# A fixed order for the first projection, the first FFN pair and the step into the down-projection, decays and residual tiles loaded earlier, and longer gaps in the weave of a one-core encoder layer

## Chip, core and metric

The kernel runs on one core of a Trainium2 chip. The metric is the device time of one execution in microseconds (us). The core has TensorE (PE, matmuls; its weight loads are listed as PEld), VectorE (DVE), ScalarE (ACT), GpSimd (POOL) and SyncE (SP). Each runs its own instructions in the order in which they were written into its list; semaphores hold an instruction until what it needs is there. SP, ACT and POOL also issue DMA transfers, and an issue stands in the engine's line like any other instruction.

## What is computed

One layer on 512 tokens of width 2048, in float32: a token mixer with eight gated-delta heads beside a gated short convolution, cross-attention to 256 memory tokens with four heads, and a SwiGLU FFN whose up-projection is followed by a causal convolution of width 3. Cut to what matters here:

```python
def gdn_group(proj, conv_w, a_log, dt_bias, out_gain):
    qkv = silu(causal_dwconv(proj[..., :3 * W], conv_w))
    q, k = l2norm(...), l2norm(...)
    beta = sigmoid(b_raw)
    g = -exp(a_log) * softplus(a_raw + dt_bias)
    o = gated_delta_rule(q, k, v, g, beta)      # decays exp(g_i - g_j), triangular solve, state over 4 chunks
    return rmsnorm(o, out_gain) * silu(z)

def memory_xattn(h, mem_n, w_q, w_k, w_v, w_o):
    q, k, v = h @ w_q, mem_n @ w_k, mem_n @ w_v
    return softmax(q @ k.T * scale) @ v @ w_o

def conv_ffn(h, w_up, conv_w, w_down):
    u = causal_dwconv(h @ w_up, conv_w)
    gate, up = u[..., :D_FF], u[..., D_FF:]
    return (silu(gate) * up) @ w_down
```

Each of the three parts has an RMSNorm ahead of it and a residual add behind it.

## The kernel before

Activations lie transposed, features on the 128 partitions and tokens along the row. A float32 product is made of three reduced ones: every operand is a rounded part (hi, made by an ACT cast) and a rest (lo, a DVE subtraction), and PE runs hi x hi, hi x lo and lo x hi into one bank of PSUM (`mm3`, L152 to L155). Weights come in pieces of 128 x 1024: SP loads a piece into one of five buffers (wst), ACT casts it to whi, DVE makes wlo (three buffers each); `wpiece` (L132) does this. So behind every matmul stands a chain of load, cast and subtraction, and an engine that stands in its line holds back the weights of everything behind it. The activations share one pool of 64 tiles (`T`). PSUM has eight banks, three in pool `PM` and five in `PG`.

The order on each engine is made by a scheduler from the program, except inside `manual_schedule`, where the named engines follow the order of the code.

The stages in order, with the times at which PE works on them:

- 0 to 74 us, keys of the memory (`mem_proj(w_xk)`, L340): 16 columns of 16 blocks, two to a tile (psk). The first tile alternates between two banks. The sum of squares of the memory tokens is built by ACT (squares) and POOL (macc, L240), and turned around by two matmuls on it (psn, L231), called from `mem_norm` behind the third tile (L326). ACT, DVE and SP follow the code for the first weight pieces (L273); PE does not. To about 400 us follow the folded query weights, the memory's values and the folded output weights.
- 400 to 1120 us, the mixer's input projection, three kinds of 16 blocks of 24 matmuls. For each head h, `qkvz` (L463) projects q, k, v and z, and behind v opens a chain (`delta`, L485) of small transposes, matmuls and vector work. `weave` and `tick` (L171 to L183) scatter the chain between the projection's matmuls: each `yield cost, gap` tells how much clock the step took and how long the next one waits, in units of about one microsecond (a block of three matmuls counts 0.65). A chain loads its row of decays (gb, L489, a DMA on POOL), forms the decay tile dt (L492), inverts a triangular matrix in steps of 16, 32 and 64 (tiles psa, bt, ps1, ps2, L566 to L593), runs over four chunks with a state (L595 to L621) and norms its output (psn, L629). The small tiles bk, nk, ss, vn come from pool `sp` with two buffers each.
- 1120 to 1395 us, the mixer's output projection and the attention scores; 1395 to 1486 us, the attention's output (`out_proj`, L748), whose 16 tiles are prepared for the FFN by `up_prepare` (L766).
- 1486 to 2382 us, the up-projection. Each of 44 pairs (a gate tile and an up tile of 128 features) is made with seven products instead of eight (a Strassen-like scheme, L836 to L884): 24 matmuls of 256 columns each, in the order r = 1, 2, 6, 5, 7, 3, 4. The weights of products 5, 6, 7 and 3 are sums of weight blocks: s1 = w21 + w22 (a second, adding DMA on POOL, L840), s3 = w21 - w11, s2 = s1 - w11 and w12 - s2 (DVE, L857 and L865). Behind the products come norm, convolution, gate, and a DMA of the hidden tile to memory (L884).
- 2390 to 2900 us, the down-projection, four groups of four output tiles (`GN`), each over 11 steps of four hidden tiles: 48 matmuls of 512 columns a step. ACT, DVE and POOL follow the code (L914). Hidden tiles (L903) and weights are split two steps or two pieces ahead. At a group's end the residual is loaded (L943, POOL), added to the bank (L944, DVE), squared (ACT) and accumulated (L240, POOL). Then the last norm and the output, to 2925 us.

Of the kernel before, what the change touches and what calls it, by code (L numbers as in the profile page):

```python
# [15 lines left out]
P = 128  # L16
S = 512
# [51 lines left out]
def trunk(ctx: ExitStack, tc: tile.TileContext, g):  # L69
# [269 lines left out]

    kts = mem_proj(g["w_xk"], True)  # L340

# [67 lines left out]
    def gates(ps):  # L409
# [17 lines left out]
        nc.vector.scalar_tensor_tensor(gr, gr, 0.0, tmp1, op0=ALU.max, op1=ALU.add)  # L427
        na = cpool.tile([P, H], F32, tag="na", name="na")
        nc.scalar.activation(na, col(C_ALOG, 8), AF.Exp)
        nc.vector.scalar_tensor_tensor(gr, gr, -1.0, rep4(na), op0=ALU.mult, op1=ALU.mult)  # L430
# [53 lines left out]

    def delta(h, q, k, v, z):  # L485
        q4, k4, v4_ = v4(q), v4(k), v4(v)

        gb = T("gb")
        nc.gpsimd.dma_start(v4(gb), gc_d[:, h, :].unsqueeze(0).broadcast_to([P, 4, P]))  # L489
        dt = T("dt")  # L490
# [79 lines left out]
        nc.scalar.copy(bt, psa)  # L570
        yield 0.5, 4.5

        for s in (32, 64):
# [3 lines left out]
            for ev, od in pairs:  # L577
                for j in range(4):
                    nc.tensor.matmul(v4(ps1)[od, j, ev], v4(nt)[ev, j, od], v4(bt)[ev, j, ev], start=True, stop=True)
# [11 lines left out]
            for ev, od in pairs:  # L591
                nc.vector.tensor_tensor(v4(pt)[ev, :, od], v4(pt)[ev, :, od], v4(ps2)[ev, :, od], op=ALU.subtract)
            yield 0.7, 2.8  # L593

        pso = PG("pso")  # L595
        st = None
        for j in range(4):
            r = v4(v)[:, j]
            if j:
                pr = PG("pr")  # L600
                nc.tensor.matmul(pr[:, :P], v4(ke)[:, j], st, start=True, stop=True)
                nc.vector.tensor_tensor(r, r, pr[:, :P], op=ALU.subtract)
                yield 0.3, 1.0
            pv = PG("pv")
            nc.tensor.matmul(pv[:, :P], v4(pt)[:, j], r, start=True, stop=True)
            vn = sp.tile([P, P], F32, tag="vn", name=nm("vn"))
            nc.scalar.activation(vn, pv[:, :P], AF.Identity, scale=bk[:, j : j + 1])
# [176 lines left out]

    turn()
    xs1 = None
    for idx in range(KT):
        n = (idx % 2) * HK + idx // 2
        out_proj(n, 0)
        out_proj(n, 1)  # L790
        ps = x2s[-1][0]
# [26 lines left out]

    def sums(s, i):

        if i == 0:
            return wp.tile([P, 1024], F32, tag="wst", name=nm(s), bufs=WST)
        return us.tile([P, 1024], F32, tag="us", name=nm(s))

    def product(ps, w, r, first):

        hi, lo = w
        for k in range(HK):
# [4 lines left out]
            nc.tensor.matmul(ps, lo[:, c], xh, start=False, stop=k == HK - 1, skip_group_check=True)  # L833

    r2 = []
    for i in range(NF):  # L836
        w11, w12, w21, w22 = (g["w_up"][q] for q in ((i, 0), (i, 1), (NF + i, 0), (NF + i, 1)))
        s1 = sums("s1", i)
        nc.sync.dma_start(s1, w21)
        nc.gpsimd.dma_start(s1, w22, accum_op=ALU.add)  # L840
        a11, a22, a12 = raw(w11), raw(w22), raw(w12)
        s3 = sums("s3", i)
        nc.scalar.activation(s3, a11, AF.Identity, scale=-1.0)
        nc.gpsimd.dma_start(s3, w21, accum_op=ALU.add)
        tt = nc.vector.tensor_tensor
        w1 = wsplit(a11)
        px = PG("px")[:, :S2]
        product(px, w1, 1, True)
        tq, tz = T("tq"), T("tz")
        nc.scalar.copy(tq[:, LO], px)  # L850
        w2 = wsplit(a12)
        py = PM("py")[:, :S2]
        product(py, w2, 2, True)
        ug, uu = T("ug"), T("uu")
        tt(ug[:, LO], py, tq[:, LO], op=ALU.add)
        s2 = sums("s2", 1)
        tt(s2, s1, a11, op=ALU.subtract)  # L857
        product(px, wsplit(s2), 6, False)
        nc.scalar.copy(tq[:, HI], px)
        pz = PG("pz")[:, :S2]  # L860
        product(pz, wsplit(s1), 5, True)
        nc.scalar.copy(tz[:, LO], pz)
        product(px, wsplit(s3), 7, False)
        tt(uu[:, HI], px, tz[:, LO], op=ALU.add)
        tt(a12, a12, s2, op=ALU.subtract)  # L865
        product(pz, wsplit(a12), 3, False)
        tt(ug[:, HI], pz, tq[:, HI], op=ALU.add)
        product(px, wsplit(a22), 4, False)
        if not r2:
            r2.append(rstd_rows([acc2]))  # L870
        tt(ug, ug, r2[0], op=ALU.mult)
        tt(uu[:, LO], px, r2[0][:, LO], op=ALU.mult)
        tt(uu[:, HI], uu[:, HI], r2[0][:, HI], op=ALU.mult)
        cvs = []
        for u, t in ((ug, i), (uu, NF + i)):
            cv = T("ucv")
            cc = C_FCONV + 3 * t
            nc.scalar.activation(cv, u, AF.Identity, scale=col(cc + 2))
            for a in (1, 2):
                nc.vector.scalar_tensor_tensor(cv[:, a:], u[:, : S - a], col(cc + 2 - a), cv[:, a:], op0=ALU.mult, op1=ALU.add)  # L880
            cvs.append(cv)
        nc.scalar.activation(cvs[0], cvs[0], AF.Silu)
        tt(cvs[0], cvs[0], cvs[1], op=ALU.mult)
        nc.scalar.dma_start(hid_d[i], cvs[0])  # L884

# [23 lines left out]
    def w_split(p):  # L909
        if p < 2 * len(steps):  # L910
            gq, c = steps[p // 2]
            ws[p] = wpiece(g["w_dn"][c, gq * GN // 2 + p % 2])

    with tc.manual_schedule(engines={mybir.EngineType.Activation, mybir.EngineType.DVE, mybir.EngineType.Pool}):  # L914
        for i in range(2):
            hid_load(i)
        for i in range(2):
            for k in range(FC):
                hid_split(i, k)
            w_split(i)  # L920
        for i, (gq, c) in enumerate(steps):
# [17 lines left out]
            if c == nc_ - 1:  # L939
                for q in range(GN):  # L940
                    n = gq * GN + q
                    x2 = T("x3")
                    nc.gpsimd.dma_start(x2, x2_d[n])  # L943
                    nc.vector.tensor_tensor(x2, pss[q], x2, op=ALU.add)  # L944
# [95 lines left out]
```

## Time and profile before

| | |
|---|---|
| time, median of three runs | 2926.73 us (2925.67 to 2928.3) |
| the profiled execution: time, span | 2926.86 us, 2925.0 us |
| PE busy, share of the span | 2832.6 us, 97% |
| mean granted clock of TensorE | 0.985 |
| DVE, ACT, POOL busy | 62%, 46%, 12% |
| DMA, mean over the span | 162 GB/s |

The span reaches from the first to the last instruction of the profiled execution. In lists of waits, `PE psd L153 <- ACT whi L142` means that PE's matmul of line 153 into psd waited for ACT's write of whi in line 142. In timelines a row gives start and duration in us, engine, line, operation, result and operands, and in brackets the idle time before it and what ended it. The granted clock is the share of full speed that TensorE was given.

### The profile page before, as it was taken

What the parts mean: (1) busy time and instruction counts of PE and PEld (TensorE: products, weight loads), DVE (VectorE), ACT (ScalarE), POOL (GpSimd) and SP (SyncE); (2) the same over time, 40 slices, a digit from 0 to 9 for tenths busy, and PEclk for the clock granted to TensorE, in tenths of its full rate; (3) what the DMA queues carried; (4) which work ended last, traced back from release to release, by engine and by line L of the source; (5) the groups of instructions that cost most, each with busy time, mean ns of one, the idle gap of its engine ahead of it and who ended that gap; (6) DMA issues with size and microseconds to landing.
All of it is one profiled execution on the core that took longest, in us unless ns stands there. A gap on an engine that the chain in (4) does not pass through costs nothing.

```text
span 2925.0 us, 44163 instructions
## 1 busy us (share of the span) xinstructions
PE 2832.6 (97%) x17521; PEld 2524.7 (86%) x17521; DVE 1820.2 (62%) x2707; ACT 1346.5 (46%) x1887; POOL 354.7 (12%) x438
## 2 busy tenths in 40 slices
PE   7999999999999999999999999999999989999996
PEld 7999888777777888888889999999999988787775
DVE  5435747767764334446678878888788774444344
ACT  5464644434443223235555555555555543433342
POOL 1020001111110000110110000000000021213132
PEclk9999999999999999999999999999999999999998
DMA  6686763323332224446666666666666665546372
GB/s 215 220 283 195 232 203 109 94 85 95 93 105 78 98 95 157 142 149 185 182 179 169 170 174 161 182 167 162 182 166 168 175 212 187 202 154 224 123 243 69
DMA packets 178944, 473.97 MB, mean 162 GB/s; under 512 B 26656, under 2 KB 50608, under 8 KB 178736
## 3 DMA queue, kind: packets, MB, share of 16 engines
q1 hardware_dynamic: 130896, 335.84, 35.1%
q0 software_dynamic: 29984, 102.80, 15.3%
q10 hardware_dynamic: 17856, 32.51, 3.0%
q8 instruction: 137, 2.24, 0.3%
q14 instruction: 71, 0.58, 0.1%
HBM read 427.02 MB, written 44.06 MB: 161 GB/s over the span
## 4 chain that ended last, share of the span: by engine, by line
PE 58%; issue 8%; DVE 3%; DMA 2%; ACT 1%; POOL 1%; ACTq 0%; SPq 0%; DVEq 0%; POOLq 0%
PE px L833 6%; PE px L831 6%; PE px L832 6%; PE psd L155 3%; PE pz L831 3%; PE pz L833 3%; PE pz L832 3%; PE psd L153 3%; PE psd L154 3%; PE pssc L153 3%; PE pssc L155 3%; PE pssc L154 3%; PE psx L154 2%; PE psx L155 2%; PE psx L153 2%
## 5 line engine op out<-in xcount | busy, mean ns | idle before, releaser
L143 DVE TENSOR_TENSOR wlo<-wst,whi 128x1024 fp32r<-128x1024 f32 x404 | 500.8, 1241 | 583.3 <-ACT whi L142 562.4
L142 ACT CAST whi<-wst 128x1024 fp32r<-128x1024 f32 x404 | 423.9, 1050 | 790.5 <-PE psd L154 237.5
L815 ACT CAST whi<-wst 128x1024 fp32r<-128x1024 f32 x176 | 184.4, 1048 | 291.4 <-PE px L832 143.8
L831 PE MATMUL px<-xoh,whi 128*128 128x256 f32 x1056 | 300.0, 284 | 3.9 <-ACT whi L815 3.2
L153 PE MATMUL psd<-hdh,whi 128*128 128x512 f32 (+1 forms) x720 | 280.4, 389 | 21.9 <-ACT whi L142 21.9
L832 PE MATMUL px<-xol,whi 128*128 128x256 f32 x1056 | 299.7, 284 | 0.0
L833 PE MATMUL px<-xoh,wlo 128*128 128x256 f32 x1056 | 299.6, 284 | 0.0
L155 PE MATMUL psd<-hdh,wlo 128*128 128x512 f32 (+1 forms) x720 | 280.2, 389 | 1.3 <-DVE wlo L143 1.2
L154 PE MATMUL psd<-hdl,whi 128*128 128x512 f32 (+1 forms) x720 | 279.6, 388 | 0.0
L816 DVE TENSOR_TENSOR wlo<-wst,whi 128x1024 fp32r<-128x1024 f32 x176 | 215.2, 1223 | 96.9 <-ACT whi L815 55.8
L831 PEld LDWEIGHTS px<-xoh,whi 128*128 128x128 f32 x1056 | 203.7, 193 | 4.3 <-ACT whi L815 3.5
L832 PEld LDWEIGHTS px<-xol,whi 128*128 128x128 f32 x1056 | 203.7, 193 | 0.0
L833 PEld LDWEIGHTS px<-xoh,wlo 128*128 128x128 f32 x1056 | 203.6, 193 | 0.0
L833 PE MATMUL pz<-xoh,wlo 128*128 128x256 f32 x704 | 199.3, 283 | 0.8 <-DVE wlo L816 0.8
L831 PE MATMUL pz<-xoh,whi 128*128 128x256 f32 x704 | 199.5, 283 | 0.2 <-ACT whi L815 0.2
L832 PE MATMUL pz<-xol,whi 128*128 128x256 f32 x704 | 199.4, 283 | 0.0
L153 PEld LDWEIGHTS psd<-hdh,whi 128*128 128x128 f32 x720 | 137.3, 191 | 50.5 <-ACT whi L142 23.3
L815 ACT CAST whi<-s 128x1024 fp32r<-128x1024 f32 x132 | 138.3, 1049 | 86.5 <-PE px L832 62.0
L155 PEld LDWEIGHTS psd<-hdh,wlo 128*128 128x128 f32 x720 | 136.9, 190 | 31.8 <-DVE wlo L143 4.5
L816 DVE TENSOR_TENSOR wlo<-s,whi 128x1024 fp32r<-128x1024 f32 x132 | 161.1, 1222 | 0.4 <-ACT whi L815 0.4
L154 PEld LDWEIGHTS psd<-hdl,whi 128*128 128x128 f32 x720 | 137.0, 190 | 27.3
L153 PE MATMUL psq<-hh,whi 128*128 128x512 f32 x384 | 155.2, 404 | 0.0
(316 smaller groups left out, 7370.2 us busy)
## 6 DMA issues: line engine op xcount, KB each, us to landing
wst<-in_w_up SPq DMA_DIRECT2D x132, 512.0 KB, 4.9
wst<-in_w_mix SPq DMA_DIRECT2D x112, 512.0 KB, 3.5
s<-in_w_up POOLq DMA_DIRECT2D x88, 512.0 KB, 6.4
wst<-in_w_dn SPq DMA_DIRECT2D x88, 512.0 KB, 3.5
hid<-hid_d POOLq DMA_DIRECT2D x176, 256.0 KB, 5.0
s<-in_w_up SPq DMA_DIRECT2D x44, 512.0 KB, 4.9
wst<-in_w_xk SPq DMA_DIRECT2D x32, 512.0 KB, 3.7
wst<-in_w_xq SPq DMA_DIRECT2D x32, 512.0 KB, 4.8
```

The lines of the kernel that those rows point to most:

```text
L142: nc.scalar.copy(hi, st)
L143: nc.vector.tensor_tensor(lo, st, f(hi), op=ALU.subtract)
L153: nc.tensor.matmul(ps, wh, xh, start=first, stop=False)
L154: nc.tensor.matmul(ps, wh, xl, start=False, stop=False)
L155: nc.tensor.matmul(ps, wl, xh, start=False, stop=last)
L815: nc.scalar.copy(hi, t)
L816: nc.vector.tensor_tensor(lo, t, f(hi), op=ALU.subtract)
L831: nc.tensor.matmul(ps, hi[:, c], xh, start=first and k == 0, stop=False, skip_group_check=True)
L832: nc.tensor.matmul(ps, hi[:, c], xl, start=False, stop=False, skip_group_check=True)
L833: nc.tensor.matmul(ps, lo[:, c], xh, start=False, stop=k == HK - 1, skip_group_check=True)
```

## The change

Five places are edited.

1. The first projection is put under `manual_schedule` for PE, and the Exp of the decay coefficients (na) moves from the gates to the start, behind the first square.

```diff
+        na = cpool.tile([P, H], F32, tag="na", name="na")
+        nc.scalar.activation(na, col(C_ALOG, 8), AF.Exp)
...
-    kts = mem_proj(g["w_xk"], True)
+    with tc.manual_schedule(engines={mybir.EngineType.PE}):
+        kts = mem_proj(g["w_xk"], True)
```

What PE's list holds around psn, before (psk is the tiles' bank, mwh and mwl the memory's two parts, macc the squares):

```order
L153 MATMUL psk_313<-mwh_151,whi_316 128x256
L154 MATMUL psk_313<-mwl_152,whi_316 128x256
L155 MATMUL psk_313<-mwh_151,wlo_317 128x256
L231 MATMUL psn_555<-macc,ones 128x256
L153 MATMUL psk_313<-mwh_161,whi_346 128x256
L154 MATMUL psk_313<-mwl_162,whi_346 128x256
L231 MATMUL psn_555<-macc,ones 128x256
L155 MATMUL psk_313<-mwh_161,wlo_347 128x256
L153 MATMUL psk_313<-mwh_161,whi_346 128x256
```

and after, where `x2` stands for two in a row:

```order
L155 MATMUL psk_438<-mwh_183,wlo_532 128x256
L153 MATMUL psk_438<-mwh_183,whi_531 128x256
L154 MATMUL psk_438<-mwl_184,whi_531 128x256
L155 MATMUL psk_438<-mwh_183,wlo_532 128x256
L231 MATMUL psn_559<-macc,ones 128x256 x2
L153 MATMUL psk_594<-mwh_129,whi_597 128x256
L154 MATMUL psk_594<-mwl_130,whi_597 128x256
L155 MATMUL psk_594<-mwh_129,wlo_598 128x256
```

The two matmuls on macc move from behind row 120 of PE's list to behind row 288, and no longer stand between others of the first tile. The first tile's 96 matmuls now alternate between its two banks.

2. A head's decays are loaded by `qkvz` behind the convolution of its first tile (of the third tile for head 0), and nine of the chain's gaps grow, two of them once for each step size and three once for each chunk.

```diff
+            if t == (0 if h else 2):
+                gb = T("gb")
+                nc.gpsimd.dma_start(v4(gb), gc_d[:, h, :].unsqueeze(0).broadcast_to([P, 4, P]))
         z = T("z")
-        weave(delta(h, *out, z), 6.0)
+        weave(delta(h, *out, z, gb), 6.0)
...
-        yield 1.4, 1.0
+        yield 1.4, 2.5
...
-        yield 0, 12.5
+        yield 0, 17.5
...
-        yield 0.5, 4.5
+        yield 0.5, 8.0
...
-            yield 0.5, 2.8
+            yield 0.5, 4.0
...
-            yield 0.7, 2.8
+            yield 0.7, 4.0
...
-                yield 0.3, 1.0
+                yield 0.3, 2.0
...
-            yield 0.3, 1.2
+            yield 0.3, 1.8
...
-            yield 0.6, 1.2
+            yield 0.6, 2.5
...
-        yield 0, 6.0
+        yield 0, 9.0
```

DVE's list where head 2's chain begins (bk_ and nt_ are head 2's, the cv_ that is subtracted from is head 0's, wlo_ are weight pieces, st_ is head 0's state), before, from head 0's last subtraction on:

```order
L602 TENSOR_TENSOR cv_4506<-cv_4506,pr_5442 128x128
L143 TENSOR_TENSOR wlo_5563<-wst_5560,whi_5562 128x1024
L564 TENSOR_TENSOR pt_5422<-xd_5420,mk 128x512
L492 SCALAR_TENSOR_TENSOR dt_5447<-gb_5445,gc,mk 128x128 x4
L530 TENSOR_TENSOR dt_5447<-pskq_5505,dt_5447 128x512
L143 TENSOR_TENSOR wlo_5621<-wst_5618,whi_5620 128x1024
L512 TENSOR_SCALAR ss_5485<-ss_5485 128x4
L520 TENSOR_TENSOR kx_5498<-pskt_5459,kd 128x512
L514 RECIPROCAL bk_5492<-ss_5485 128x4
L515 TENSOR_TENSOR bk_5492<-bk_5492,beta 128x4
L523 SCALAR_TENSOR_TENSOR nt_5500<-pskk_5464,bk_5492,dts_5457 128x128 x4
```

and after:

```order
L604 TENSOR_TENSOR cv_4509<-cv_4509,pr_5575 128x128
L143 TENSOR_TENSOR wlo_5672<-wst_5669,whi_5671 128x1024
L619 SCALAR_TENSOR_TENSOR st_5631<-st_5555,egl,pss_5629 128x128
L604 TENSOR_TENSOR cv_4509<-cv_4509,pr_5651 128x128
L143 TENSOR_TENSOR wlo_5755<-wst_5752,whi_5754 128x1024
L516 RECIPROCAL bk_5471<-ss_5464 128x4
L517 TENSOR_TENSOR bk_5471<-bk_5471,beta 128x4
L525 SCALAR_TENSOR_TENSOR nt_5479<-pskk_5430,bk_5471,dts_5423 128x128 x4
L539 TENSOR_TENSOR nd_5520<-nt_5479,mk 128x512
```

Head 2's reciprocal now follows head 0's last subtraction with one weight piece between them; the same pair of neighbours comes back with the other heads.

3. Around the attention's output the weights are cast one tile ahead (`out_piece`), and the first pair's loads, its first two casts and its two sums of weight blocks are written ahead of the last output tile. The first s2 takes the buffer of w11 in place of one of its own. Later pairs do the same work as before, their loads through `pair_loads`.

```diff
+        if idx == KT - 2:
+
+            a11, a12, a22, s1, s3 = pair_loads(0, lambda t: wp.tile([P, 1024], F32, tag="wst", name=nm(t), bufs=WST))
+            first = [a11, a12, a22, s1, s3]
+        out_proj(0)
+        out_proj(1)
+        if idx == KT - 1:
+            first += [wsplit(a11), wsplit(a12)]
+            tt(a11, s1, a11, op=ALU.subtract)
+            tt(a12, a12, a11, op=ALU.subtract)
```

ACT's list at the last output tile (x_d is the DMA of the residual to memory, xs the scaled tile, xoh its parts for the products, tq a product's copy; the casts from s_ are of sums of weight blocks), before:

```order
L795 DMA x_d<-x_2117_12763 128x512
L239 ACTIVATE sq_12767<-x_2117_12763 128x512
L798 ACTIVATE xs_12770<-x_2117_12763,cols 128x512
L148 CAST xoh_12780<-xs_12770 128x512
L148 CAST xoh_12784<-tc_12772 128x512
L148 CAST xoh_12788<-td_12773 128x512
L850 COPY tq_12837<-px_12812 128x256
L815 CAST whi_12874<-s_2143_12872 128x1024
L815 CAST whi_12904<-s_2128_12796 128x1024
L815 CAST whi_12933<-s_2132_12805 128x1024
```

and after:

```order
L784 CAST b11h_12685<-xs_12751 128x256
L803 CAST whi_12878<-wst_12710 128x1024
L803 CAST whi_12908<-s_2112_12707 128x1024
L840 DMA x_d<-x_2126_12788 128x512
L239 ACTIVATE sq_12792<-x_2126_12788 128x512
L843 ACTIVATE xs_12795<-x_2126_12788,cols 128x512
L148 CAST xoh_12805<-xs_12795 128x512
L148 CAST xoh_12809<-tc_12797 128x512
L148 CAST xoh_12813<-td_12798 128x512
L926 COPY tq_12847<-px_12822 128x256
L803 CAST whi_12937<-s_2116_12716 128x1024
```

Two casts of sums (of s2, which now lies in a wst buffer, and of s1) move ahead of the last tile's square and scaling. In SP's list the load of the second pair's s1 moves from the first place of that pair's loads to the third, behind two weight loads; in DVE's list the second pair's s2 now stands ahead of the sum uu of the first.

4. The last pair and the first steps of the down-projection get one written order on ACT and DVE, and the hidden tiles of the first two steps are loaded behind the last pair's first product.

```diff
+        with tc.manual_schedule(engines={mybir.EngineType.Activation, mybir.EngineType.DVE}):
+            product(px, wsplit(s3), 7, False)
+            tt(a12, a12, s2, op=ALU.subtract)
+            product(pz, wsplit(a12), 3, False)
+            w4 = wsplit(a22)
             for k in range(FC):
...
+                hid_split(0, k)
+            tt(uu[:, HI], px, tz[:, LO], op=ALU.add)
+            product(px, w4, 4, False)
+            w_split(0)
+            tt(ug[:, HI], pz, tq[:, HI], op=ALU.add)
+            w_split(1)
+            gate = gate_half(i, ug)
+            for k in range(FC):
+                hid_split(1, k)
+            up_half(i, px, uu, gate)
```

`gate_half` and `up_half` hold what each pair did before in one piece: norm, convolution (`unit_conv`) and SiLU of the gate, then norm and convolution of the other half, the product and the DMA of the hidden tile.

5. The residual tiles of a group are loaded at its eighth step of eleven, and only added at its end.

```diff
             hid_load(i + 2)
+            if c == NC_ - 4:
+                for q in range(GN):
+                    x3.append(T("x3"))
+                    nc.gpsimd.dma_start(x3[-1], x2_d[gq * GN + q])
...
-                    x2 = T("x3")
-                    nc.gpsimd.dma_start(x2, x2_d[n])
-                    nc.vector.tensor_tensor(x2, pss[q], x2, op=ALU.add)
-                    x3.append(x2)
+                    nc.vector.tensor_tensor(x3[n], pss[q], x3[n], op=ALU.add)
                     if gq < KT // GN - 1:
-                        add_squares(acc3, x2, n == 0)
+                        add_squares(acc3, x3[n], n == 0)
```

On POOL the four loads then stand ahead of the hidden tiles of three further steps, and the group's four accumulations one behind the other.

More of the change, by code (lines that the diff above doesn't have):

```diff
@@ L427, in gates @@
         nc.vector.scalar_tensor_tensor(gr, gr, 0.0, tmp1, op0=ALU.max, op1=ALU.add)
-        na = cpool.tile([P, H], F32, tag="na", name="na")
-        nc.scalar.activation(na, col(C_ALOG, 8), AF.Exp)
         nc.vector.scalar_tensor_tensor(gr, gr, -1.0, rep4(na), op0=ALU.mult, op1=ALU.mult)
@@ L483, in four, with delta @@
             nc.tensor.matmul(v4(ps)[:, j], lhs(j), rhs(j), start=True, stop=True)
-    def delta(h, q, k, v, z):
+    def delta(h, q, k, v, z, gb):
         q4, k4, v4_ = v4(q), v4(k), v4(v)
-        gb = T("gb")
-        nc.gpsimd.dma_start(v4(gb), gc_d[:, h, :].unsqueeze(0).broadcast_to([P, 4, P]))
         dt = T("dt")
@@ L745, in trunk, with out_piece, out_proj @@
     HK = KT // 2
-    x2s = []
-    def out_proj(n, part):
+    x2s, x2w = [], []
+    order2 = [(i % 2) * HK + i // 2 for i in range(KT)]
+    def out_piece():
+        n = order2[len(x2w)]
+        x2w.append(wpiece(mo_d[:, :, n * P : (n + 1) * P].rearrange("k p n -> p k n")))
+    def out_proj(part):
         if part == 0:
-            x2s.append((PM("psx2"), *wpiece(mo_d[:, :, n * P : (n + 1) * P].rearrange("k p n -> p k n"))))
-        ps, hi, lo = x2s[-1]
+            x2s.append(PM("psx2"))
+        ps, (hi, lo) = x2s[-1], x2w[len(x2s) - 1]
         for k in range(4 * part, 4 * part + 4):
@@ L783, in up_prepare, with raw, wsplit, pair_loads @@
             xop[right].append((th[:, HI], tl[:, HI]))
+    tt = nc.vector.tensor_tensor
+    def raw(src):
+        t = wp.tile([P, 1024], F32, tag="wst", name=nm("wst"), bufs=WST)
+        nc.sync.dma_start(t, src)
+        return t
+    def wsplit(t):
+        hi = wp.tile([P, 1024], F32R, tag="whi", name=nm("whi"))
+        lo = wp.tile([P, 1024], F32R, tag="wlo", name=nm("wlo"))
+        nc.scalar.copy(hi, t)
+        nc.vector.tensor_tensor(lo, t, f(hi), op=ALU.subtract)
+        return hi, lo
+    def pair_loads(i, buf):
+        w11, w12, w21, w22 = (g["w_up"][q] for q in ((i, 0), (i, 1), (NF + i, 0), (NF + i, 1)))
+        s1 = buf("s1")
+        nc.sync.dma_start(s1, w21)
+        nc.gpsimd.dma_start(s1, w22, accum_op=ALU.add)
+        a11, a22, a12 = raw(w11), raw(w22), raw(w12)
+        s3 = buf("s3")
+        nc.scalar.activation(s3, a11, AF.Identity, scale=-1.0)
+        nc.gpsimd.dma_start(s3, w21, accum_op=ALU.add)
+        return a11, a12, a22, s1, s3
     turn()
+    out_piece()
     xs1 = None
     for idx in range(KT):
[L788 to L791, printed above, removed]
+        n = order2[idx]
+        if idx + 1 < KT:
+            out_piece()
+        if idx == KT - 2:
[7 more added lines that the diff above has]
+            tt(a12, a12, a11, op=ALU.subtract)
+        ps = x2s[-1]
         x1 = TB("x2")
@@ L805, in trunk, with US @@
     us = ctx.enter_context(tc.tile_pool(name="us", bufs=4, reuse_waits="tile"))
-    def raw(src):
-        t = wp.tile([P, 1024], F32, tag="wst", name=nm("wst"), bufs=WST)
-        nc.sync.dma_start(t, src)
-        return t
-    def wsplit(t):
-        hi = wp.tile([P, 1024], F32R, tag="whi", name=nm("whi"))
-        lo = wp.tile([P, 1024], F32R, tag="wlo", name=nm("wlo"))
-        nc.scalar.copy(hi, t)
-        nc.vector.tensor_tensor(lo, t, f(hi), op=ALU.subtract)
-        return hi, lo
[L819 to L823, printed above, removed]
+    def US(t):
+        return us.tile([P, 1024], F32, tag="us", name=nm(t))
     def product(ps, w, r, first):
@@ L833, in product @@
             nc.tensor.matmul(ps, lo[:, c], xh, start=False, stop=k == HK - 1, skip_group_check=True)
[L835 to L884, printed above, removed]
     NC_ = NF // FC
@@ L912, in w_split, with unit_conv @@
             ws[p] = wpiece(g["w_dn"][c, gq * GN // 2 + p % 2])
-    with tc.manual_schedule(engines={mybir.EngineType.Activation, mybir.EngineType.DVE, mybir.EngineType.Pool}):
[L915 to L920, printed above, removed]
+    r2 = []
+    def unit_conv(u, t):
+        cv = T("ucv")
+        cc = C_FCONV + 3 * t
+        nc.scalar.activation(cv, u, AF.Identity, scale=col(cc + 2))
+        for a in (1, 2):
+            nc.vector.scalar_tensor_tensor(cv[:, a:], u[:, : S - a], col(cc + 2 - a), cv[:, a:], op0=ALU.mult, op1=ALU.add)
+        return cv
@@ new lines, in gate_half, with up_half @@
+    def gate_half(i, ug):
+        tt(ug, ug, r2[0], op=ALU.mult)
+        cv = unit_conv(ug, i)
+        nc.scalar.activation(cv, cv, AF.Silu)
+        return cv
+    def up_half(i, px, uu, gate):
+        tt(uu[:, LO], px, r2[0][:, LO], op=ALU.mult)
+        tt(uu[:, HI], uu[:, HI], r2[0][:, HI], op=ALU.mult)
+        cv = unit_conv(uu, NF + i)
+        tt(gate, gate, cv, op=ALU.mult)
+        nc.scalar.dma_start(hid_d[i], gate)
+    for i in range(NF):
+        if i:
+            a11, a12, a22, s1, s3 = pair_loads(i, US)
+            w1 = wsplit(a11)
+        else:
+            a11, a12, a22, s1, s3, w1, w2 = first
+        px = PG("px")[:, :S2]
+        product(px, w1, 1, True)
+        if i == NF - 1:
+            hid_load(0)
+            hid_load(1)
+        tq, tz = T("tq"), T("tz")
+        nc.scalar.copy(tq[:, LO], px)
+        if i:
+            w2 = wsplit(a12)
+        py = PM("py")[:, :S2]
+        product(py, w2, 2, True)
+        ug, uu = T("ug"), T("uu")
+        tt(ug[:, LO], py, tq[:, LO], op=ALU.add)
+        if i:
+            s2 = US("s2")
+            tt(s2, s1, a11, op=ALU.subtract)
+        else:
+            s2 = a11
+        product(px, wsplit(s2), 6, False)
+        nc.scalar.copy(tq[:, HI], px)
+        pz = PG("pz")[:, :S2]
+        product(pz, wsplit(s1), 5, True)
+        nc.scalar.copy(tz[:, LO], pz)
+        if i < NF - 1:
+            product(px, wsplit(s3), 7, False)
+            tt(uu[:, HI], px, tz[:, LO], op=ALU.add)
+            if i:
+                tt(a12, a12, s2, op=ALU.subtract)
+            product(pz, wsplit(a12), 3, False)
+            tt(ug[:, HI], pz, tq[:, HI], op=ALU.add)
+            product(px, wsplit(a22), 4, False)
+            if not r2:
+                r2.append(rstd_rows([acc2]))
+            up_half(i, px, uu, gate_half(i, ug))
+            continue
+        with tc.manual_schedule(engines={mybir.EngineType.Activation, mybir.EngineType.DVE}):
+            product(px, wsplit(s3), 7, False)
+            tt(a12, a12, s2, op=ALU.subtract)
+            product(pz, wsplit(a12), 3, False)
+            w4 = wsplit(a22)
+            for k in range(FC):
+                hid_split(0, k)
+            tt(uu[:, HI], px, tz[:, LO], op=ALU.add)
+            product(px, w4, 4, False)
+            w_split(0)
+            tt(ug[:, HI], pz, tq[:, HI], op=ALU.add)
+            w_split(1)
+            gate = gate_half(i, ug)
+            for k in range(FC):
+                hid_split(1, k)
+            up_half(i, px, uu, gate)
```

## The prediction

> **What bounds the kernel now.** I start with the page's busy times, because they say how much there is to win at all.
>
> ```profile
> PE 2832.6 (97%) x17521; PEld 2524.7 (86%) x17521; DVE 1820.2 (62%) x2707; ACT 1346.5 (46%) x1887; POOL 354.7 (12%) x438
> ```
>
> TensorE (PE) is busy for 2832.6 of 2925.0 us, so the span is its work plus 92 us of idle time, plus what its throttled clock costs after a pause. No other engine comes near. The change keeps every product, so it can win only in those pauses. The waits of PE name them (total, times, longest).
>
> ```profile
> PE psd L153 <- ACT whi L142: 21.9, 4, 7.8
> PE psn L231 <- POOL macc L240: 7.6, 1, 7.6
> ...
> PE ps L579 <- ACT bt L570: 4.7, 1, 4.7
> PE ps L579 <- DVE bt L590: 3.8, 2, 2.5
> PE px L831 <- ACT whi L815: 3.2, 1, 3.2
> ...
> PE psn L630 <- ACT snh L148: 2.1, 3, 0.8
> ...
> PE psa L568 <- DVE y L635: 1.5, 1, 1.5
> ...
> PE psk L155 <- DVE wlo L143: 0.8, 1, 0.8
> ```
>
> All but the last hold 44.8 us. To see what a pause costs with the slow clock behind it, I count matmuls. In the window view (us; busy time and count of PE, PEld, DVE, ACT, POOL; granted clock; DMA share; GB/s) a stretch without a pause holds 211 matmuls of 256 columns in 25 us (0.119 us each) or 112 of 512 columns (0.223 us each). A stretch that holds fewer has lost the difference times that step.
>
> ```profile
> 25.00:50.00 25.00, 17.43 (x130) 16.87 (x129) 12.92 (x17) 11.04 (x13) 10.12 (x7) 0.86 0.37 121
> 50.00:75.00 25.00, 25.00 (x211) 25.00 (x210) 14.76 (x20) 10.72 (x12) 0.00 (x0) 1.00 0.64 214
> 500.00:600.00 100.00, 99.17 (x561) 80.08 (x561) 74.81 (x210) 40.09 (x67) 7.34 (x7) 1.00 0.32 97
> 600.00:700.00 100.00, 94.31 (x525) 75.32 (x525) 66.32 (x149) 45.78 (x79) 16.92 (x14) 0.97 0.33 95
> 700.00:800.00 100.00, 97.37 (x525) 78.83 (x524) 76.30 (x206) 45.77 (x79) 14.93 (x14) 1.00 0.31 91
> 800.00:925.00 125.00, 120.05 (x671) 94.99 (x669) 81.33 (x215) 48.45 (x79) 10.65 (x10) 0.96 0.30 92
> 1475.00:1500.00 25.00, 21.12 (x110) 17.80 (x109) 19.31 (x28) 15.19 (x23) 6.34 (x6) 0.90 0.52 143
> 1500.00:1525.00 25.00, 23.46 (x187) 23.06 (x186) 17.42 (x24) 15.89 (x21) 2.55 (x3) 0.96 0.70 184
> ...
> 2375.00:2400.00 25.00, 17.11 (x94) 14.66 (x93) 16.82 (x24) 11.59 (x20) 9.08 (x17) 0.80 0.82 279
> 2500.00:2525.00 25.00, 24.23 (x107) 19.71 (x106) 7.79 (x11) 8.07 (x13) 3.90 (x5) 1.00 0.25 84
> 2525.00:2550.00 25.00, 23.96 (x103) 19.20 (x104) 15.44 (x19) 13.44 (x21) 15.31 (x28) 1.00 0.93 353
> 2550.00:2575.00 25.00, 25.00 (x112) 20.71 (x111) 11.73 (x15) 8.96 (x14) 4.79 (x9) 1.00 0.72 251
> 2625.00:2650.00 25.00, 21.61 (x96) 17.57 (x94) 6.84 (x9) 6.65 (x11) 5.33 (x6) 0.97 0.24 72
> 2650.00:2675.00 25.00, 21.51 (x82) 16.98 (x83) 14.25 (x17) 13.77 (x21) 14.10 (x25) 0.82 0.80 300
> 2775.00:2800.00 25.00, 18.43 (x69) 14.19 (x68) 13.23 (x17) 11.69 (x17) 13.64 (x23) 0.80 0.66 244
> ```
>
> **Part A, the first projection in program order.** PE reaches the sum of squares of the memory tokens (psn) after 120 matmuls and stands, since POOL is still adding the squares.
>
> ```profile
> 34.31 1.22 PE L231 MATMUL psn<-macc,ones 128*128 128x256 f32 x2 [7.57 <-POOL macc L240]
> ...
> 22.09 12.16 POOL L240 TENSOR_TENSOR macc<-macc,sq 128x512 f32<-128x512 f32 x7 [21.64 <-ACT sq L239]
> ```
>
> Lost in 25 to 50: (211 - 130) x 0.119 = 9.6 us. PE came to it at 34.3 - 7.6 = 26.7. In the new order 288 matmuls stand ahead of psn, 168 more, or 20 us; PE then asks for it at about 47 us and the adds end at 34.3, so that the wait has 12 us to spare. The weight pieces of those 168 matmuls have to be cast earlier, and ACT is free to do so from 25 us on. What is new is the order within the first 192 matmuls: the two banks of the first tile alternate, so PE needs the second weight piece sooner; I charge 0.6 us for that, somewhat less than the wait for a weight piece in the last row above. **A: 9 us, between 7 and 10.** The Exp of the decay coefficients also moves behind the casts; it takes 0.2 us either way.
>
> **Part B, decays early and longer gaps in the weave.** The four windows from 500 to 925 hold 425.0 - 410.9 = 14.1 us of idle PE, and the clock there is short by 0.03 x 100 + 0.04 x 125 = 8.0 us, some of which lies on the idle time itself. The largest wait has its root on POOL.
>
> ```profile
> 609.03 0.77 POOL L489 DMA_DIRECT2D gb<-gc_d  x1
> ...
> 615.04 1.14 DVE L492 SCALAR_TENSOR_TENSOR dt<-gb,gc,mk 128x128 f32<-128x128 f32 x4 [4.26 <-DMA gb<-gc_d]
> ...
> 625.13 0.57 ACT L570 COPY bt<-psa 128x512 f32<-128x512 f32 x1
> ```
>
> The decay row (gb) is fetched when the chain wants it; DVE stands 4.26 us, everything behind it is late, and ACT copies bt at 625.13, where PE has waited 4.7 us. Loaded a tile earlier, the row is there. The other three rows of the waits (bt by DVE, snh, y: 3.8, 2.1, 1.5) are waits of a step on one that stood too near; their gaps grow from 2.8 to 4.0, 6.0 to 9.0 and 12.5 to 17.5 clock units (one unit is about 1 us of projection). Together 12.1 us. I take three quarters, 9 us, and 2 us of clock. Against it stands the length of a chain: its gaps grow by 28.4 units, from 91.5 (own matmuls not counted) to 119.9, while a new head starts about every 52. Two chains were open at a time, now for a while three, and the small tiles (bk, nk, vn) have two buffers. In the new DVE order the reciprocal of head h+2 stands one weight piece behind the last subtraction of head h: it waits for head h's last vn, and the weight subtractions stand in line behind it. One weight piece lasts 24 x 0.227 = 5.4 us (the step of the 2550 window), which covers a short stand. **B: 11 us, between -10 and 20.**
>
> **Part C, the sums of the first pair in weight blocks.** The first matmuls of the up-projection and its wait:
>
> ```profile
> 1485.45 0.28 PE L831 MATMUL px<-b11h,whi 128*128 128x256 f32 x1
> ...
> 1495.47 2.94 ACT L815 CAST whi<-s 128x1024 fp32r<-128x1024 f32 x3 [2.33 <-DVE s L857]
> ...
> 1503.78 1.22 DVE L857 TENSOR_TENSOR s<-s,wst 128x1024 f32<-128x1024 f32 x1 [3.67 <-DMA s<-in_w_up]
> ...
> 1492.80 0.33 SPq L839 DMA_DIRECT2D s<-in_w_up  x1
> ```
>
> Up to 1485.45 the window from 1475 has room for 47 matmuls at 0.223, behind it for 122 at 0.119: 169, and 110 were issued, so 7.0 us are lost; the next window loses (211 - 187) x 0.119 = 2.9. In the new order s2 is made, cast and split ahead of the last tile, so the 3.2 us wait and the slow clock behind it go. New: ACT casts s1 ahead of the last tile's scaling and waits for the buffer that the first product holds, which makes the last tile about 1 us late. And the second pair's s1, once first in SP's line, now stands behind two weight loads; it took 11.0 us from issue (1492.80) to use (1503.78). Issued at about 1494 it is there at 1505, DVE's s2 of pair 2 (1.22) now stands ahead of the sum that frees the bank for product 4, PE comes to product 4 after six products of 24 matmuls, at 1485.45 + 144 x 0.119 + 1.0 = 1503.6, and waits about 2 us. Another 0.8 us goes to a copy behind a longer cast. 9.9 - 1.0 - 2 - 0.8 = 6; **C: 5 us, between 0 and 6.5**, a little less because the two waits can also open the clock's loss again.
>
> **Part D, the order into the down stage.** ACT casts the first hidden tiles only behind the last pair's gate:
>
> ```profile
> 2387.42 2.18 ACT L148 CAST hdh<-hid 128x512 fp32r<-128x512 f32 x4 [2.69 <-DVE ucv L883]
> ...
> 2382.47 0.28 PE L833 MATMUL px<-xoh,wlo 128*128 128x256 f32 x1
> ```
>
> The products end at 2382.6; the window has room for 64 + 78 matmuls and holds 94, so 48 x 0.223 = 10.7 us are lost (7.8 of them the longest whi wait). Hidden tiles 0 to 7 and the down weights depend on nothing of the last pair. Written ahead of it, four casts of 0.55 (2.18 in all) and three weight casts of 1 us (2.94 for three in part C) fit into ACT's gaps between the last four products, 4 x 24 x 0.119 = 11 us, and the subtractions into DVE's. The gate now comes after them, but its result is needed only in the 11th step. **D: 10 us, between 8 and 11.**
>
> **Part E, residual tiles loaded four steps ahead.** At a group's end POOL loads a tile, DVE adds, ACT squares, POOL accumulates, and only then comes POOL's next load:
>
> ```profile
> 2642.02 0.55 POOL L943 DMA_DIRECT2D x<-x_d  x1
> 2646.59 1.25 POOL L240 TENSOR_TENSOR acc<-acc,sq 128x512 f32<-128x512 f32 x1 [4.02 <-ACT sq L239]
> ...
> 2645.08 0.69 DVE L944 TENSOR_TENSOR x<-psd,x 128x512 f32<-128x512 f32 x1 [5.12 <-DMA x<-x_d]
> ```
>
> Three such rounds of 5.7 us hold ACT's next weight cast. The losses of the three boundaries are (224 - 210), (224 - 178) and (112 - 69) matmuls: 103 x 0.223 = 23.0 us. With the tiles in place DVE's four additions (0.69 each) follow the banks, ACT squares beside them, and the casts are at most 3 us late with a step of 10.9 us (48 x 0.227) in hand. The loads themselves, 1 MB a group, fall into a stretch with DMA share 0.72. **E: 22 us, between 17 and 23.**
>
> The Trainium skill, "TensorE: Matmul & The Clock Gate", Part 1, ties the half clock to an idle window of about 3.4 us and lets it go after as much work. By that rule E would bring its idle time, 14.1 us (21.9 less D's 7.8), plus half of 3.4 for each of two boundaries, an estimate of 17.5 us. The counts of this trace give 23.0, so I keep the count; by the rule the time would be about 2875.
>
> **Sum.** 9 + 11 + 5 + 10 + 22 = 57. Span 2925.0 - 57 = 2868; the profiled execution took 2926.86, 1.86 more than its span and 0.13 over the median 2926.73, so the time is **2870 us**. With all upper bounds (10 + 20 + 6.5 + 11 + 23 = 70.5) it is 2856; with all lower ones (7 - 10 + 0 + 8 + 17 = 22) 2905, which would need all five to fail at once.
>
> **Rivals.**
> First, B wins nothing or loses: three open chains on two buffers make new waits of the size of those removed. For it speaks the DVE order above, against it that DVE is busy for 66 to 76 of 100 us there. The others bring 46: 2881, and up to 2891 with ten lost.
> Second, only the idle time comes back and the slow clock stays where it was for reasons of its own: 7.6 + 9 + 3.2 + 7.8 + 14.1 = 41.7, or 2885. Against it: the clock is 1.00 in the windows without a pause.
> Third, C falls to its new wait: product 4 waits 5 us instead of 2 and the clock drops behind it, so C brings nothing: 2875.
> Fourth, the change doesn't do what it says at a group boundary: the hidden-tile loads behind the early tile loads find no free buffer, POOL stands, and E is worth a third: 2885.
> Fifth, slower. The place is the reciprocal of head h+2 in the six heads that follow two others. ACT's waits for that product:
>
> ```profile
> ACT vn L607 <- PE pv L605: 65.3, 25, 5.9
> ```
>
> If each head stands for the longest, 5.9 us, past its cover, and pays a throttled stretch like that of the 2650 window (0.18 x 25 = 4.5), 6 x 10.4 = 62 us are lost against 46 gained: 2943. It decides from (46 + 5.9) / 6 = 8.7 us a head; today one head of eight shows more than 4 us.
>
> **How the numbers follow.** Forecast as summed 0.62 (2856 to 2880); B nothing or lost 0.18; clock 0.05; C to its wait 0.06; E by a third 0.04; slower chains 0.03; and 0.02 for a mixture that ends where it began. The range takes in the first four: 2855 to 2893. A measurement of this kernel tells 0.2% (5.9 us) from no change: faster 0.95, same 0.02, slower 0.03.
>
> **What would show it.** A: psn behind the third tile, no wait at 26 to 34, 211 matmuls in 25 to 50 save a few. B: no wait of ps on bt above 1 us, gb landed long before dt; wrong if bk or nt become the longest releasers on DVE. C: no wait for whi of s; a wait before product 4 of the first pair of 2 us. D: the down stage starts within 1 us of the last product, clock 1.00. E: four accumulations back to back on POOL and about 112 matmuls in every window of the three boundaries. I am wrong most easily in B, whose bounds are the widest, and then in C.

## The result, and the profile after

The changed kernel takes 2902.9 us (median of four runs, 2900.3 to 2906.9) against 2926.2 before: a ratio of 0.9921, 95% interval 0.9904 to 0.9938. It is faster by 23 us where 57 were forecast, and lies outside the range. First the waits of PE in the changed kernel (total, times, longest in us), the same view as before, without the wait for the first memory tile (7.8 us) and that of the last norm (7.2 us), which the kernel before has too.

```profile
...
PE ps L581 <- ACT ww L582: 7.0, 4, 3.1
PE pr L603 <- DVE dt L532: 5.8, 3, 2.5
PE psq L153 <- DVE z L483: 5.6, 1, 5.6
PE px L859 <- DVE uu L945: 4.8, 1, 4.8
...
PE pv L607 <- DVE dt L532: 1.9, 1, 1.9
PE ps L581 <- ACT bt L572: 1.9, 1, 1.9
```

The waits of A, D and E (psn for macc, psd for whi) are not in the list any more. In their place stand waits of the weave (ps, pr, pv, and psq, which the chains hold up) and one of the first pair (px for uu). The window view shows the same by counts of matmuls, PE's first.

```profile
25.00:50.00 25.00, 24.98 (x206) 24.67 (x205) 16.46 (x11) 11.87 (x13) 10.99 (x7) 1.00 0.62 210
...
500.00:925.00 425.00, 399.15 (x2173) 321.14 (x2173) 292.62 (x763) 171.15 (x287) 49.38 (x41) 0.97 0.30 90
1475.00:1500.00 25.00, 24.48 (x129) 20.89 (x127) 21.23 (x30) 15.02 (x24) 6.94 (x5) 1.00 0.46 131
1500.00:1525.00 25.00, 18.49 (x127) 17.43 (x127) 14.91 (x20) 13.86 (x19) 4.03 (x4) 0.86 0.80 220
2375.00:2400.00 25.00, 25.00 (x178) 23.47 (x178) 19.04 (x25) 13.23 (x20) 9.09 (x17) 1.00 0.74 270
...
2625.00:2650.00 25.00, 25.00 (x112) 20.69 (x111) 13.85 (x17) 14.28 (x23) 16.14 (x23) 1.00 0.58 201
```

A: 206 matmuls where there were 130, so 76 x 0.119 = 9.0 us came back. D and E: PE is busy without a break over both places, at full clock; the windows of the other two boundaries hold 112 matmuls each as well. The weave is the surprise. The same stretch of the kernel before:

```profile
500.00:925.00 425.00, 410.90 (x2277) 329.21 (x2276) 298.76 (x779) 180.09 (x302) 49.84 (x44) 0.98 0.31 94
```

PE is idle for 25.9 us instead of 14.1 and issues 104 matmuls fewer. At 425 / 2277 = 0.187 us each that is about 19 us lost, an estimate, since the windows are not cut at the same place of the program. And the first pair lost its old wait and got one of 4.8 us with the clock at 0.86 behind it. By this estimate the missing 34 us (57 - 23) split into about 30 in part B (11 forecast, 19 lost) and 4 to 6 in part C.

At a group's end POOL now accumulates in one piece (start, duration):

```profile
2631.06 6.28 POOL L240 TENSOR_TENSOR acc<-acc,sq 128x512 f32<-128x512 f32 x4 [41.31 <-ACT sq L239]
```

Four additions in 6.28 us, with no load between them, as part E had it.

### The profile page after: what moved, and what is told of

Its sections match the earlier page's. It is cut to its first block, busy times and chain, and to the rows that moved or that the text cites. A ratio compares the mean times of both kernels' runs of the same rounds, so it can differ in the third digit from the quotient of the medians.

```text
span 2901.3 us, 44142 instructions
## 1 busy us (share of the span) xinstructions
PE 2825.3 (97%) x17521; PEld 2523.0 (87%) x17521; DVE 1827.7 (63%) x2707; ACT 1347.0 (46%) x1887; POOL 361.1 (12%) x438
## 4 chain that ended last, share of the span: by engine, by line
PE 81%; issue 7%; DVE 4%; DMA 4%; ACT 2%; POOL 2%; ACTq 0%; SPq 0%; DVEq 0%; POOLq 0%
PE px L859 6%; PE px L860 6%; PE px L861 6%; PE psd L154 5%; PE psd L155 5%; PE psd L153 5%; PE pssc L153 3%; PE pssc L155 3%; PE pssc L154 3%; PE pz L861 3%; PE pz L859 3%; PE pz L860 3%; PE psx L154 2%; PE psx L155 2%; PE psx L153 2%
```

## The experiments

Theory one: the longer gaps let a third chain begin while the first still runs; its reciprocal (bk of head h+2) then has to wait for the last vn of head h, because bk has two buffers, and what stands behind it comes late. The rivals: the early load of the decays costs by itself; three chains crowd PSUM and the engines' lines whatever the buffers; or the loss isn't in part B at all.

### Part B taken apart

**Part B as before, the rest as changed.**

```diff
-            if t == (0 if h else 2):
-                gb = T("gb")
-                nc.gpsimd.dma_start(v4(gb), gc_d[:, h, :].unsqueeze(0).broadcast_to([P, 4, P]))
...
-        yield 0, 17.5
+        yield 0, 12.5
```

> Parts A, C, D and E as changed, part B as before: the decay row is loaded by the chain itself and the nine gaps have their old lengths. If part B costs what the counts of the two profiles say (about 15 us more lost between 400 and 1025 us than before), this runs in about 2887 us. If B is neutral and the missing time lies elsewhere, it stays at 2903; if B gains 11 us as the prediction had it, it takes 2914.

Measured 2884.5 us (ratio 0.9857, 0.9842 to 0.9871). Part B therefore costs 18 us in the changed kernel; it doesn't gain 11.

**Old gaps, early decays.**

```diff
-        yield 1.4, 2.5
+        yield 1.4, 1.0
...
-        yield 0, 9.0
+        yield 0, 6.0
```

> The changed kernel with the nine gaps of the weave at their old lengths; the early load of the decays stays. Theory one (the longer gaps make a third chain overlap, and that costs): 2880 to 2888 us, below the kernel with all of B undone by the 4 to 8 us that the early decays bring. Theory two (the early load costs, by its place on GpSimd's list or the tile it holds): no better than 2900.

2883.7 us (0.9854, 0.9840 to 0.9869). The loss goes with the gaps. The early decays, from which I expected 4 to 8 us, bring nothing that can be told against 2884.5, though DVE no longer waits for them. The largest wait of the weave, PE for ACT's bt, falls from 4.7 to 1.4 us, but the waits for DVE's bt and y grow from 4.0 to 5.8 and from 1.3 to 2.6.

**Long gaps, late decays.**

```diff
-            if t == (0 if h else 2):
-                gb = T("gb")
-                nc.gpsimd.dma_start(v4(gb), gc_d[:, h, :].unsqueeze(0).broadcast_to([P, 4, P]))
...
+    def delta(h, q, k, v, z):
...
+        gb = T("gb")
+        nc.gpsimd.dma_start(v4(gb), gc_d[:, h, :].unsqueeze(0).broadcast_to([P, 4, P]))
```

> The changed kernel with the decays loaded by the chain itself, as before; the nine gaps stay long. Theory one (the gaps cost): 2903 to 2912 us, with VectorE's wait for the decays back at 4 us for some heads. Theory two (the early load costs): about 2887.

2911.0 us (0.9948, 0.9933 to 0.9963): 8 us slower than the changed kernel. The runs don't overlap (2908.0 to 2913.1 against 2900.3 to 2906.9), though the two intervals just touch. With the long gaps the early load doesn't cost, then, and seems to help, so the rival that it costs is out. VectorE's wait for the decays, which I expected back, isn't among its waits; the loss shows as longer waits of PE for z (13.7 us in three, against 5.6 in one). How the late load leads to them is not shown.

**Four buffers for the small tiles.**

```diff
-    sp = ctx.enter_context(tc.tile_pool(name="sp", bufs=2))
+    sp = ctx.enter_context(tc.tile_pool(name="sp", bufs=4))
```

> The changed kernel with four buffers instead of two for the small tiles (bk, nk, ss, vn, st), so that the reciprocal of head h+2 need not wait for the last vn of head h. If the two buffers are the root of the loss in the weave: 2883 to 2892 us, VectorE's waits of tm for ab (19 us in the changed kernel) down to about 9. If the three chains crowd each other otherwise (PSUM banks, VectorE's and ScalarE's line), 2898 to 2905 with most of these waits still there.

2875.8 us (0.9825, 0.9808 to 0.9841): 27 us off, more than B had lost. One part of the expectation failed, and is taken up below: VectorE still waits 18.9 us for ab.

**Four buffers for bk alone.**

```diff
-        bk = sp.tile([P, 4], F32, tag="bk", name=nm("bk"))
+        bk = sp.tile([P, 4], F32, tag="bk", name=nm("bk"), bufs=4)
```

> The changed kernel with four buffers for bk alone; ss, nk, vn and st keep two. If the reciprocal that waits for a buffer of bk is the whole of it, the time is that of the kernel with four buffers for all small tiles (2876 us, within 5). If the other small tiles matter as well, it lies between 2880 and 2900.

2877.2 us (0.9829, 0.9815 to 0.9842), the same as with four for all, and the lists of DVE and PE are the same row for row. The buffers of one tile of 128 x 4 numbers hold the whole loss of part B.

**Four buffers in the kernel before.**

```diff
-    sp = ctx.enter_context(tc.tile_pool(name="sp", bufs=2))
+    sp = ctx.enter_context(tc.tile_pool(name="sp", bufs=4))
```

> The kernel before with four buffers for the small tiles and nothing else. By the theory that two buffers bind only when the longer gaps make a third chain overlap, nothing changes: 2924 to 2929 us. If the two buffers bound the old weave too, 2910 to 2920.

2926.5 against 2926.0 us (1.0001, 0.9991 to 1.0010), as theory one has it: with the old weave two buffers cost nothing.

**Four buffers with the old gaps.**

> Four buffers for the small tiles, early decays, but the old gap lengths. If the longer gaps are worth something once the buffers are there: 2883 us, as with two buffers and old gaps, 7 us over 2876. If four buffers help the old gaps just as well, and the longer ones are worth nothing: 2872 to 2877.

The edits are the two shown for old gaps and for four buffers. 2880.2 us (0.9842, 0.9829 to 0.9856), between the two forecasts. The long gaps bring 4.4 us over this, but the intervals of the two overlap; it stays open whether gaps alone are worth anything. The same holds for four buffers with the old gaps, 3.5 us (2883.7 against 2880.2). Of B's 8.7 us with four buffers (2884.5 - 2875.8) no single edit is shown to hold a definite share.

How the buffer reaches PE can be read at heads 2 and 3 (counted from 0). DVE's waits in the changed kernel from 420 to 960 hold only little for bk itself:

```profile
DVE tm L557 <- DMA ab<-nd_d: 19.1, 6, 6.0
...
DVE bk L516 <- ACT vn L609: 4.1, 4, 1.1
```

The cost lies in where the reciprocal stands in DVE's list. Timeline of DVE in the changed kernel, head 2 first and then head 3:

```profile
543.42 0.16 DVE L514 TENSOR_SCALAR ss<-ss 128x4 f32<-128x4 f32 x1
...
563.36 0.17 DVE L516 RECIPROCAL bk<-ss 128x4 f32<-128x4 f32 x1
...
613.87 0.61 DVE L514 TENSOR_SCALAR ss<-ss 128x4 f32<-128x4 f32 x1
...
621.56 0.29 DVE L604 TENSOR_TENSOR cv<-cv,pr 128x128 f32<-128x128 f32 x1 [0.58 <-PE pr L603]
622.93 0.18 DVE L516 RECIPROCAL bk<-ss 128x4 f32<-128x4 f32 x1 [1.08 <-ACT vn L609]
...
625.23 1.05 DVE L541 TENSOR_REDUCE ndc<-nd 128x128 f32<-128x512 f32 x1
626.19 1.22 DVE L143 TENSOR_TENSOR wlo<-wst,whi 128x1024 fp32r<-128x1024 f32 x1
632.24 0.29 DVE L557 TENSOR_TENSOR tm<-ab,xb 128x124 f32<-128x124 f32 x1 [4.83 <-DMA ab<-nd_d]
632.45 0.68 DVE L483 SCALAR_TENSOR_TENSOR z<-z,psz 128x512 f32<-128x512 f32 x1
```

and PE at its largest wait there:

```profile
633.18 0.80 PE L153 MATMUL psq<-hh,whi 128*128 128x512 f32 x1 [5.58 <-DVE z L483]
```

In head 2 the reciprocal comes 20 us behind ss, with two subtractions of head 0 between them. In head 3 the sum ss is ready at 614.5 and the reciprocal runs at 622.9, behind head 1's last subtraction and its vn. Only then come nt, nd and ndc, which go to memory and back as ab. Behind one weight piece tm stands 4.83 us for ab, and z stands behind tm; PE needs the bank that z reads. With four buffers the same rows of head 3, and PE's wait behind them, are:

```profile
595.80 0.60 DVE L514 TENSOR_SCALAR ss<-ss 128x4 f32<-128x4 f32 x1
...
596.92 0.16 DVE L516 RECIPROCAL bk<-ss 128x4 f32<-128x4 f32 x1
...
613.43 0.29 DVE L557 TENSOR_TENSOR tm<-ab,xb 128x124 f32<-128x124 f32 x1 [7.24 <-DMA ab<-nd_d]
...
615.08 0.79 PE L607 MATMUL pv<-cv,pt 128*128 128x128 f32 x2 [3.53 <-DVE cv L604]
```

1.1 us from ss to bk instead of 9.1. And ss itself comes 18 us earlier, though PE reaches head 3's products pskk only 2.9 us earlier (586.36 against 589.28): most of the delay lies in the order of DVE's list and not in DVE's stand for vn. DVE still stands 7.24 us for ab: that wait doesn't go with the buffers, and my expectation was wrong to name it as the sign. Behind it PE now waits 3.53 us for cv instead of 5.58 for z. Over the whole stretch from 500 to 925 PE's idle time falls to 10.2 us.

```profile
500.00:925.00 425.00, 414.85 (x2314) 337.51 (x2313) 307.41 (x772) 179.63 (x298) 47.31 (x43) 0.98 0.31 95
```

That bk's buffers are the cause is shown by the one-tile edit. How the loss divides between the wait on the chip and the other order into which the scheduler writes all engines' rows is not: both change with the edit, and no run has the old order with more buffers. Head 3 speaks for the order as the larger share.

### Part C

**Part C as before, with four buffers.**

```diff
-        if idx == KT - 2:
-            a11, a12, a22, s1, s3 = pair_loads(0, lambda t: wp.tile([P, 1024], F32, tag="wst", name=nm(t), bufs=WST))
...
-        if idx == KT - 1:
-            first += [wsplit(a11), wsplit(a12)]
-            tt(a11, s1, a11, op=ALU.subtract)
-            tt(a12, a12, a11, op=ALU.subtract)
...
+        s2 = US("s2")
+        tt(s2, s1, a11, op=ALU.subtract)
```

> Four buffers, and part C as before: weights of the attention's output not cast ahead, first pair's sums behind the last tile. If part C took away one wait and put another of the same size in its place: 2873 to 2878 us, with the 3.2 us wait for the cast of s2 back. If C brought 5 us as predicted: 2881.

2877.9 us (0.9831, 0.9818 to 0.9845): no difference from 2875.8 that can be told. The old wait is back at 3.2 us and the new one gone. In the changed kernel the new one reads, on SP, POOL, DVE and PE:

```profile
1504.57 0.33 SPq L811 DMA_DIRECT2D s<-in_w_up  x1
...
1508.61 0.85 POOL L812 DMA_DIRECT2D s<-in_w_up  x1 [0.82 <-DMA s<-in_w_up]
...
1518.02 1.23 DVE L935 TENSOR_TENSOR s<-s,wst 128x1024 f32<-128x1024 f32 x1 [6.73 <-DMA s<-in_w_up]
1519.16 0.42 DVE L945 TENSOR_TENSOR uu<-px,tz 128x256 f32<-128x256 f32 x1
...
1519.72 0.55 PE L859 MATMUL px<-xoh,whi 128*128 128x256 f32 x1 [4.85 <-DVE uu L945]
```

The second pair's s1 is issued at 1504.57, when the last tile's rests are split, and its second, adding transfer takes from 1508.61 to 1518.0. DVE stands 6.73 us for it, with uu behind.

**The second pair's s1 added by POOL.**

```diff
-        nc.gpsimd.dma_start(s1, w22, accum_op=ALU.add)
+        if i != 1:
+            nc.gpsimd.dma_start(s1, w22, accum_op=ALU.add)
         a11, a22, a12 = raw(w11), raw(w22), raw(w12)
+        if i == 1:
+            nc.gpsimd.tensor_tensor(s1, s1, a22, op=ALU.add)
```

> Four buffers, and the second pair's s1 is made by a GpSimd addition of the block w22 that is loaded anyway, in place of the adding DMA. By the theory that part C's gain is eaten by product 4 of the first pair, which waits 4.85 us through the late s1 and pays slow clock behind it: s1 is there about 5 us earlier, the wait falls below 1 us and the time to about 2867 (8 to 9 us less than 2876). If the wait only moves to the next product, 2873 to 2877.

2868.9 us (0.9808, 0.9795 to 0.9822), 6.9 less than with the buffers alone, and the fastest of all. The intervals of the two still overlap, so the place itself has to show it. Its waits of PE over the first two pairs:

```profile
PE pz L864 <- DVE wlo L804: 1.3, 2, 0.9
PE px L862 <- ACT tq L929: 1.0, 1, 1.0
PE px L862 <- ACT tq L942: 0.9, 1, 0.9
```

No wait for uu is left (5.7 us with the buffers alone), and the clock is 1.00. The window with the buffers alone, and with POOL's addition:

```profile
1475.00:1500.00 25.00, 18.34 (x127) 17.48 (x127) 14.23 (x20) 12.97 (x16) 2.66 (x4) 0.86 0.76 213
...
1475.00:1500.00 25.00, 22.25 (x182) 21.64 (x180) 21.78 (x27) 17.04 (x22) 4.97 (x4) 1.00 0.71 181
```

From the first product to the first matmul of the third pair PE takes 50.1 us with part C as before (from 1470.34), 51.5 with part C (from 1467.38) and 45.4 with POOL's addition (from 1463.03). So part C's gain was there, and one transfer took it back.

### Parts A, D and E, each taken out of the kernel with four buffers

```diff
-    with tc.manual_schedule(engines={mybir.EngineType.PE}):
-        kts = mem_proj(g["w_xk"], True)
+    kts = mem_proj(g["w_xk"], True)
```

> Four buffers, and the first projection's order left to the scheduler again: by the counts of the two profiles A is worth 9 us, so 2885; the wait of psn for macc is back at 7 to 8 us in 25 to 50 us.

2881.8 us (0.9855, 0.9841 to 0.9870), 6 over 2875.8. Its runs spread from 2880.9 to 2889.3, so the place says more than the time. The count in its own profile:

```profile
25.00:50.00 25.00, 17.39 (x127) 16.81 (x126) 12.52 (x16) 11.08 (x13) 10.11 (x7) 0.86 0.36 116
```

(206 in the changed kernel - 127) x 0.119 = 9.4 us. The last matmul into psk, which comes before the weave, agrees: it starts at 303.8 us here and at 294.6 with part A, 9.2 us earlier (305.3 and 296.2 in the kernels before and after).

```diff
-        if i == NF - 1:
-            hid_load(0)
-            hid_load(1)
...
+        for i in range(2):
+            hid_load(i)
+        for i in range(2):
+            for k in range(FC):
+                hid_split(i, k)
+            w_split(i)
```

> Four buffers, and the step into the down stage as before (hidden tiles loaded and split behind the last pair): by the counts D is worth 10.6 us, so 2887, with one wait of 7 to 8 us for whi at the stage's start.

2885.4 us (0.9860, 0.9845 to 0.9875), 9.7 over, with the wait of 7.8 us for whi back.

```diff
-            if c == NC_ - 4:
-                for q in range(GN):
-                    x3.append(T("x3"))
-                    nc.gpsimd.dma_start(x3[-1], x2_d[gq * GN + q])
...
+                    x3.append(T("x3"))
+                    nc.gpsimd.dma_start(x3[n], x2_d[n])
```

> Four buffers, and the residual tiles loaded at the group's end as before: by the counts E is worth 22 us, so 2898, with three waits for whi at the group boundaries, 14 us together.

2897.6 us (0.9905, 0.9890 to 0.9919), 21.8 over, with three waits for whi of 14.5 us together.

## Why the prediction was wrong, step by step

| part | forecast | measured | from |
|---|---|---|---|
| A | +9 | +9 | counts and the last psk, 9.0 to 9.4; taken out, four buffers: 6.0 |
| B | +11 (-10 to 20) | -18 | taken out, two buffers: 2884.5 - 2902.9 |
| C | +5 (0 to 6.5) | about 0 | taken out, four buffers: 2877.9 against 2875.8 |
| D | +10 | +9.7 | taken out, four buffers |
| E | +22 | +21.8 | taken out, four buffers |

9 - 18 + 0 + 10 + 22 = 23, the gain that was measured: the parts add up, and the miss lies in B and C.

**A, D and E** were right in mechanism and size. Counting matmuls against a window without a pause gave the sizes, slow clock included: E's count of 23.0 us lies near the 21.8 measured. The estimate of 17.5 us by the Trainium skill, "TensorE: Matmul & The Clock Gate", Part 1, lies below it.

**B** failed in its sign. The step that failed is the price of the buffer wait: against it the prediction set only that one weight piece lasts 5.4 us, "which covers a short stand", charged nothing, and took three quarters of the removed waits as gain. I had the place (the reciprocal of head h+2 behind head h's last subtraction) and the two buffers, but priced only DVE's stand. That is 4.1 us over four heads, so the sign I had named, bk among the longest releasers on DVE, did not show. What it cost was the delay of all that hangs on the reciprocal: 20 us from ss to bk in head 2 and 9.1 in head 3, then the round trip of nd through memory, then z and the banks. Instead of the 11 us gained, 18 were lost, below my lower end of -10, though far short of the 62 of the fifth rival. It is the mechanism of the first and the fifth rival, with a size between theirs (ten lost, 62 lost).

A second step failed too. The decays were the root of the largest wait, which fell from 4.7 to 1.4 us, but the removed waits were taken as gained time. With the early load alone other waits grew, and the time fell by 0.8 us, which can't be told from nothing.

**C** failed in the size of the new wait. The prediction has product 4 wait "about 2 us" and takes 1 us off for the slow clock. Measured were 4.85 us, and a granted clock of 0.86 in the window, which lost (211 - 127) x 0.119 = 10.0 us. Two errors made it longer: s1 is issued 11.2 us behind the first product (1504.57 against 1493.39), not about 8 (1494, with the first product at 1485.45 and up to 1 us late), and takes 13.4 us to its use, not 11.0. The third rival (the new wait eats C) is what happened; it had 0.06.

The chances were off with it: 0.62 stood on the forecast as summed, 0.18 on B bringing nothing or losing at most ten, and 0.03 on slower chains. Two small slips change no term: the gaps of a chain add up to 93.3 units before and 121.7 after, its first wait of 6.0 included, and not to 91.5 and 119.9; and the step of the 2550 window is 0.223 us, while 0.227 is that between rows of the timeline.

## What to carry to other kernels

When a schedule is stretched so that more instances of a chain are open at once, count the buffers of every tile that lives through the chain, the smallest too: here two more buffers of a 128 x 4 tile turned a loss of 18 us into a gain of about 7 (2877.2 against 2884.5). Price a buffer wait by what depends on the waiting result and by where it puts the instruction in its engine's list, not by how long the engine stands. And where a wait is removed ahead of a stage, follow the next stage's loads to the same moment: one late transfer gave part C's gain back until it was replaced.

## What the runs showed of the hardware

Short pauses cost more than themselves. In the kernel before PE stood 2.54 us for bt (by DVE) from 869.23 to 871.77, the longest of those waits. The window view around it, cut where the granted clock changes (the third number from the end), has:

```profile
866.00:870.38 4.38, 3.23 (x40) 2.00 (x39) 0.38 (x2) 1.30 (x2) 0.00 (x0) 1.00 0.46 133
870.38:880.62 10.24, 8.85 (x32) 6.90 (x33) 6.60 (x17) 1.46 (x3) 0.00 (x0) 0.50 0.30 100
880.62:884.00 3.38, 3.38 (x21) 2.73 (x21) 2.11 (x9) 0.60 (x2) 0.00 (x0) 1.00 0.00 0
```

The clock fell to one half 1.15 us into the pause and came back only at 880.62, after PE had worked for 8.85 us without a break. The Trainium skill, "TensorE: Matmul & The Clock Gate", Part 1, has about 3.4 us for both; here the pause was shorter and the slow stretch longer. In all fourteen profiles of this case the trace's record of the granted clock, apart from the first 14 and the last 30 us, has stretches at half clock of 3.41, 6.83 or 10.24 us only: one, two or three times the same length.
